# RWKV's triangular inverses from diagonal blocks of 16 rows, joined to 32 rows on TensorE

## The chip, the cores and the metric

The kernel runs on one core of one Trainium2 chip. The metric is device time in microseconds (us), the median of several runs. The engines are named as in the profile: PE is TensorE (PEld its weight loads), DVE is VectorE, ACT is ScalarE, POOL is GpSimd, and SP issues DMAs.

## The reference

One encoder layer is computed for 256 tokens of width 2048 in float32: a normalisation, one wide projection, three mixers (gated MLP, Hyena long convolutions, RWKV-7 in both directions), a gated merge, an output projection and a feed-forward network. The change lies in the RWKV mixer alone. It has 16 heads of 64 channels, and for each head and direction this recurrence over the tokens:

```python
def step(s, inp):
    r_t, w_t, k_t, v_t, a_t, b_t = inp
    sa = jnp.einsum('dbhij,dbhj->dbhi', s, a_t)
    s = s * w_t[..., None, :] + sa[..., :, None] * b_t[..., None, :] + v_t[..., :, None] * k_t[..., None, :]
    return s, jnp.einsum('dbhij,dbhj->dbhi', s, r_t)
```

The kernel takes it in four chunks of 64 tokens. Inside a chunk the term with `sa` makes a triangular system I - M of 64 x 64, whose inverse is needed; between chunks a state of 64 x 64 for each head and direction is carried.

## The kernel before

Products with the large weights are "dense" steps: a piece of weights, 128 x 512, is loaded by SP into `w`, split by ACT into a high part `wh` (L225) and by DVE or POOL into a low part `wl` (L229), and PE then makes three matmuls for each 128 rows (L242, L243, L244, into `ps_dn`).

The RWKV stage goes over eight pairs of heads, j = 0 to 7. For each j five generators write code, and `threads` takes turns between them:

- `wkv_prep`: decays and scaled keys (`bk`, `ar`, `E`), with the scans on DVE (L555, L557) and products of POOL (L590 to L594);
- `wkv_scores`: score products on PE (L635), masked by DVE into `sc` (L637). ACT copies the 32 x 32 blocks on the diagonals into `Md` (L647), DVE transposes those of the second direction into `Mu` (L649), and SP writes both to a DRAM tile `d1`;
- `wkv_inverse`: it loads the 32 blocks of 32 x 32 back into `N` so that a block lies on one partition (four copies of the 32 blocks fill the 128 partitions), and inverts them by substitution. For each of 31 rows DVE makes one product into `Yt` (L688) and one sum into `Y` (L689), each quarter of the partitions for every fourth row of the result. `Y` goes to a DRAM tile `d2` and returns as `XX`, which DVE transposes (L702);
- `wkv_chain`: it joins the 32-row inverses to 64-row ones by two products (L731, an ACT copy L734, L742; DVE writes `xf`, L722 and L747), and then goes through the four chunks. Each has the products L770 (and L777 from the second chunk on) on PE, a copy `Pm` by DVE (L780), the product with the inverse L785, copies to `UV` (L791), state products L796, new state `sb` by DVE (L811, L813), and output products L816 and L819, summed in `y` (L826);
- `wkv_norm`: the group norm (L842, L843, ACT's L846, L848) and the gate.

After each turn in which a generator had something to do, `threads` puts dense steps into the code, about four for a round (12 matmuls): the projections of the j that come next (`front`), and, where the queue is short, the merge products of the Hyena branch. `need` puts in all that is left of a projection before the j that takes it. What is left when the generators are done is run behind them. `after` orders the generators among each other: the scores of j wait for the chain of j - 2, and a chain for its own inverse. The order of the instructions on each engine is then set by a scheduler, which takes the order of the code as priority and may move an instruction ahead of others that it holds to be late.

Of the kernel before, what the change touches and what calls it, by code (L numbers as in the profile page):

```python
# [9 lines left out]
F32 = mybir.dt.float32  # L10
# [6 lines left out]
P = 128  # L17
T = 256
D = 2048
KD = D // P  # L20
# [28 lines left out]
for _n, _w in VEC:  # L49
# [6 lines left out]
    ("smask", 256), ("dmask", 64), ("rowm", 2), ("scanm", 257),  # L56
# [11 lines left out]
def shape_constants():  # L68
    c = [np.zeros((P, NCST), np.float32), np.zeros((P, NCSW), np.float32)]

    def put(name, a):
        a = np.asarray(a, np.float32).reshape(P, -1)
        o, n, w = COFF[name]
        c[w][:, o:o + n] = a

    p = np.arange(P)
    put("ident", np.eye(P))
    put("bones", (p[:, None] // 64 == p[None, :] // 64) / 64.0)
    put("ones", np.full((P, P), 1.0 / D))
    put("unit", np.ones((P, P)))  # L80
    s = (p % 64)[:, None]
    t = np.arange(64)[None, :]
    put("smask", np.concatenate([s < t, s <= t, s > t, s >= t], 1))
    blk = (p // 32) % 2
    put("dmask", (np.arange(2)[None, :, None] == blk[:, None, None]) * np.ones((1, 1, 32)))
    put("rowm", np.stack([blk == 0, blk == 1], 1))
    put("scanm", np.broadcast_to((np.arange(T + 1) % CH != 0)[None], (P, T + 1)))
    lin = linspace01()
    put("negt", np.broadcast_to(-lin[None], (P, T)))
    return c  # L90
# [18 lines left out]
def dft_tables():  # L109
    """odd frequencies (2 k + 1) pi / (2 T), k < T / 2; even and odd samples apart"""  # L110
    n = np.arange(T).reshape(P, 2, 1, 1)
    k = np.arange(P)
    th = np.pi * (2 * k + 1) * n / (2 * T)
    fwd = np.concatenate([np.cos(th), -np.sin(th)], 2)
    inv = (fwd / T).transpose(3, 2, 1, 0)
    return tuple(np.ascontiguousarray(a.reshape(P, 512), dtype=np.float32) for a in (fwd, inv))
# [15 lines left out]
def layout(inp):  # L132
    g = {k: np.asarray(v) for k, v in inp.items()}
    o = {}
# [52 lines left out]
    o["rows"] = np.eye(32).reshape(8, 4, 32).transpose(1, 0, 2)[:, None] * np.ones((1, 32, 1, 1))  # L187
    o["rows"] = o["rows"].reshape(P, 8, 32)
# [5 lines left out]
class Build:  # L194
# [21 lines left out]
    # weights [P, nk, n] from DRAM -> (wh, wl)  # L216
# [16 lines left out]
    def dense(self, ap, xh, xl, ps):  # L233
        """ps[n, t] = sum_k w[k, n] x[k, t]; ap DRAM [P, nk, 128], xh/xl [P, nk, 256]; yields after each k"""
        mm = self.nc.tensor.matmul
        nk = ap.shape[1]
        for k0 in range(0, nk, KPIECE):
            k1 = min(nk, k0 + KPIECE)
            wh, wl = self.take(ap[:, k0:k1, :])
            for k in range(k0, k1):  # L240
                i = k - k0
                mm(ps, wh[:, i, :], xh[:, k, :], start=(k == 0), stop=False)  # L242
                mm(ps, wh[:, i, :], xl[:, k, :], start=False, stop=False)  # L243
                mm(ps, wl[:, i, :], xh[:, k, :], start=False, stop=(k == nk - 1))  # L244
                yield

    def dense_wide(self, ap, x, ps, whole=False):
        """as dense, in fewer passes: x(k) is [P, 2, 256], the two parts, and the sum of ps's halves the product;
        with whole it is in the first half"""
        mm = self.nc.tensor.matmul  # L250
        nk = ap.shape[1]
        for k0 in range(0, nk, KPIECE):
            k1 = min(nk, k0 + KPIECE)
            wh, wl = self.take(ap[:, k0:k1, :])
            for k in range(k0, k1):
                i = k - k0
# [12 lines left out]
    def take(self, ap):  # L269
        """the split weights; those that the plan has next are split ahead of their turn"""  # L270
# [6 lines left out]
    def feed(self, label, gen, aps):  # L277
        """gen takes the weights aps, [P, nk, 128] each, one after the other"""
# [4 lines left out]
    def fill(self, n):  # L283
        """emits n steps of the waiting dense products"""
# [26 lines left out]
    def rsqrt_steps(self, x, w, v):  # L311
        """w * -RS_B = x ** -0.5 (x > 0): bit estimate and two Newton steps"""
# [74 lines left out]
    def rwkv(self, rp, ych, ycl, y):  # L387
# [9 lines left out]
        # kd = k (1 + (a - 1) k_a) = k (ka1 (2 a - 1) + ka0)  # L397
# [19 lines left out]

        fronts = {}
# [15 lines left out]
        def more():  # L434
            """the next merge, the queue being short"""
# [45 lines left out]
    def threads(self, live, more):  # L481
        """takes turns between the generators, with dense steps between: more where fewer have something to do"""
# [19 lines left out]
    def weave(self, gens, steps, lead=0):  # L502
        """takes turns between the generators (a pair (n, gen) starts n turns late), with some of `steps` dense ones between"""
# [22 lines left out]
    def wkv_prep(self, R, j, front, res):  # L526
        """decay, a, normalised k; what scores and chain take; bonus and gate"""
# [11 lines left out]
        # cum = sum of sigmoid(w) from the chunk's edge, ta = 2 sigmoid(a) - 1  # L539
# [19 lines left out]
        # normalised kk, with its sign turned  # L559
# [39 lines left out]
        # bonus  # L599
# [18 lines left out]
    def wkv_scores(self, R, j, pre, sts):  # L618
        """scores of all chunks; transposed b, k; the blocks to invert"""
# [7 lines left out]
        # scores  # L627
# [11 lines left out]
        # the 32 x 32 blocks on the diagonals of M, upper (for d = 1 transposed)  # L639
# [10 lines left out]
        d1 = self.dp.tile([2, 4, P, 32], F32, tag="d1", name="d1", bufs=2)  # L650
        for d, z in enumerate((Md[:, 0, :], Mu)):
            nc.sync.dma_start(d1[d].rearrange("u p e -> p u e"), z.rearrange("p (u e) -> p u e", e=32))
        sts[j] = [sc, d1]
        self.passed.add(("blocks", j))
        yield 1
        # transposed b, k
# [10 lines left out]
    def wkv_inverse(self, R, j, st):  # L667
        """inverses of the diagonal 32 x 32 blocks of I - M, with a block on a partition: the partitions hold four times the
        32 blocks, each time with every fourth row of the inverses"""
        rp = R["rp"]  # L670
        V, D = self.nc.vector, self.nc.sync
        tl = lambda sh, name, bufs=1: rp.tile([P] + sh, F32, tag=name, name=name, bufs=bufs)
        mult, add = ALU.mult, ALU.add
        d1 = st[1]
        N = tl([32, 32], "N")
        yield 1
        src = d1.rearrange("d u (q s) e -> (d u q) (s e)", s=32)
        for i in range(4):
            D.dma_start(N[32 * i:32 * i + 32].rearrange("p s e -> p (s e)"), src)
        Y, Yt = tl([8, 32], "Y"), tl([80], "Yt")  # L680
# [3 lines left out]
        E = self.nc.vector  # L684
        for k in range(31):
            n, w = 31 - k, k // 4 + 1
            z = Yt[:, :w * n].rearrange("p (c t) -> p c t", t=n)
            E.tensor_tensor(z, N[:, k, k + 1:].unsqueeze(1).broadcast_to([P, w, n]), Y[:, :w, k:k + 1].broadcast_to([P, w, n]), mult)  # L688
            E.tensor_tensor(Y[:, :w, k + 1:], Y[:, :w, k + 1:], z, add)  # L689
            if k % 4 == 3:  # L690
                yield 1
        d2 = self.dp.tile([32, 8, 4, 32], F32, tag="d2", name="d2", bufs=2)
        for i in range(4):
            D.dma_start(d2[:, :, i, :], Y[32 * i:32 * i + 32])
        yield 1
        yield from self.after("whole", j - 1)
        # [transposed d = 0, inverse d = 1, inverse d = 0, transposed d = 1]
        XX = tl([4, P], "XX")
        D.dma_start(XX[:, :2].rearrange("p d (u e) -> p (d u) e", e=32), d2.rearrange("(u q) c r e -> (q c r) u e", q=4))
        yield 1  # L700
        yield 1
        V.transpose(XX[:, 2:].rearrange("p a b -> p (a b)"), XX[:, :2].rearrange("p a b -> p (a b)"))  # L702
# [4 lines left out]
    def wkv_chain(self, R, j, pre, st):  # L707
        """the inverses of the 64 x 64 blocks, the chain over chunks"""
# [7 lines left out]
        sc, _, bkT, XX = st  # L716
# [33 lines left out]
        # v in [t, channel] layout, next to where u will stand  # L750
# [11 lines left out]
        # chain over chunks  # L762
# [70 lines left out]
    def wkv_norm(self, R, j, pre, ych, ycl):  # L833
        """group norm, bonus and gate"""
# [28 lines left out]
    def filter_mlp(self, p, zs):  # L863
        """z3[hidden, t] of the implicit filters' network: high parts, and low parts below them"""
# [37 lines left out]
    def filter_weights(self, p, o, g):  # L902
        """high parts twice, for both parts of z3, and low parts; after the load"""
# [14 lines left out]
    def filter_block(self, p, z3, edec, o, g, nxt, out):  # L918
        """spectra (E + O, E - O of even and odd taps) of 256 channels' filters, the skip as a part of tap 0"""
# [56 lines left out]
    def plus_minus(self, p, out, ps):  # L976
        """out[:, 0 / 1] = ps[0] +- ps[1], [re, im] each"""
# [13 lines left out]
    def tables(self, p):  # L991
        """the transforms' tables and the first filters' weights"""
# [138 lines left out]
    def gmlp(self, p, yah, yal):  # L1131
        """spatial gating; its products take x g, their results the token's 1 / rms; on the way h, for the others"""
# [28 lines left out]
        # the functions' table is there before the first data  # L1161
# [101 lines left out]
    def merge_part(self, p, n, b, y, out, first):  # L1263
        """out[:, n] (+)= (1 + tanh(gate / 2)) (y w_branch): twice the branch's term"""
# [54 lines left out]
    def sumsq(self, p, acc, x, n):  # L1319
        """acc += x ** 2 (and the mean's epsilon), but for the last of the KD tiles, which is returned"""  # L1320
# [10 lines left out]
    def token_rstd(self, p, acc, nm, last):  # L1331
        """r * -RS_B is the tokens' 1 / rms"""
# [66 lines left out]
```

## Time and profile before

| what | value |
|---|---|
| median of 3 runs | 2072.45 us (2071.43 to 2075.77) |
| span of the profiled execution | 2081.1 us |
| PE, PEld busy | 95%, 85% |
| DVE, ACT, POOL busy | 71%, 49%, 27% |

The profile is one execution, whose span is 8.7 us above the median of the runs. A busy PE is not a PE at its peak: a matmul of 256 columns is shown with some 0.28 us though the next one starts 0.12 us after it. The RWKV stage, from the first matmul of its preparation to the last norm and the dense steps behind it, lies between 509 and 1110 us; before it come the gated MLP and Hyena, after it the merge, the output projection and the feed-forward network.

### The profile page before, as it was taken

The numbers are of one execution on the slowest core, as the hardware profiler recorded it, in microseconds if no ns is written. First come the engines' busy times: TensorE is split into PE (matmuls) and PEld (weight loads), VectorE is DVE, ScalarE is ACT, GpSimd is POOL, SyncE is SP. The second block draws the span as 40 slices with busy tenths as digits, with TensorE's granted clock in tenths as the row PEclk, the third lists the DMA queues.
The fourth block names the chain that finished last, engine by engine and source line by source line (L and its number), as shares of the span: only waits on it lengthen the run. The fifth ranks groups of instructions, "written<-read, shape, count | busy, mean of one in ns | idle before, by whom it ended". The sixth has DMA issues, their size and how long they took to land. (4 is left out here: it accounts for less than half of the span.)

```text
span 2081.1 us, 37899 instructions
## 1 busy us (share of the span) xinstructions
PE 1985.2 (95%) x13636; PEld 1762.9 (85%) x13636; DVE 1468.4 (71%) x2852; ACT 1020.5 (49%) x1982; POOL 552.9 (27%) x557
## 2 busy tenths in 40 slices
PE   7999999999888888999999999999999999999997
PEld 5899999999777777877778888888888888888886
DVE  7968788765887786776766667766666666655555
ACT  5655555545333343333335555555555555544543
POOL 5322322325643443453441121111111111100001
PEclk9999999999888999898899999999999999999998
DMA  7454444345332233332324556555555555566664
GB/s 235 153 173 151 133 161 150 127 157 175 121 103 84 86 106 94 106 103 74 107 91 161 186 197 219 186 191 189 192 189 191 189 190 190 190 186 187 186 187 137
DMA packets 200325, 324.35 MB, mean 156 GB/s; under 512 B 45766, under 2 KB 49352, under 8 KB 200136
## 3 DMA queue, kind: packets, MB, share of 16 engines
q1 hardware_dynamic: 193904, 310.33, 45.9%
q0 software_dynamic: 1888, 5.93, 0.9%
q10 hardware_dynamic: 4344, 5.67, 0.8%
q8 instruction: 107, 1.75, 0.4%
q14 instruction: 82, 0.67, 0.1%
HBM read 317.65 MB, written 4.19 MB: 155 GB/s over the span
## 5 line engine op out<-in xcount | busy, mean ns | idle before, releaser
L225 ACT CAST wh<-w 128x512 fp32r<-128x512 f32 x1148 | 705.0, 619 | 693.8 <-PE ps_dn L262 259.6
L229 DVE TENSOR_TENSOR wl<-w,wh 128x512 fp32r<-128x512 f32 x945 | 709.0, 755 | 370.0 <-ACT wh L225 366.2
L242 PE MATMUL ps_dn<-hw,wh 128*128 128x256 f32 x1328 | 407.4, 307 | 2.3 <-ACT th L1269 1.2
L229 POOL TENSOR_TENSOR wl<-w,wh 128x512 fp32r<-128x512 f32 x203 | 273.2, 1349 | 454.7 <-ACT wh L225 432.2
L244 PE MATMUL ps_dn<-hw,wl 128*128 128x256 f32 x1328 | 388.8, 293 | 1.3 <-DVE wl L229 1.3
L243 PE MATMUL ps_dn<-hw,wh 128*128 128x256 f32 x1328 | 389.7, 293 | 0.0
L242 PEld LDWEIGHTS ps_dn<-hw,wh 128*128 128x128 f32 x1328 | 264.5, 199 | 18.6 <-issue 8.5
L243 PEld LDWEIGHTS ps_dn<-hw,wh 128*128 128x128 f32 x1328 | 265.1, 200 | 4.3 <-issue 1.7
L244 PEld LDWEIGHTS ps_dn<-hw,wl 128*128 128x128 f32 x1328 | 264.7, 199 | 3.7 <-DVE wl L229 1.5
L262 PE MATMUL ps_dn<-gw,wh 128*128 128x512 f32 x704 | 246.3, 391 | 0.0
L262 PE MATMUL ps_big<-gw,wh 128*128 128x512 f32 x704 | 246.0, 391 | 0.0
L262 PE MATMUL ps_dn<-hid,wh 128*128 128x512 f32 x660 | 233.2, 396 | 0.0
L263 PE MATMUL ps_dn<-hid,wl 128*128 128x256 f32 x704 | 198.4, 282 | 0.0
L263 PE MATMUL ps_dn<-gw,wl 128*128 128x256 f32 x704 | 197.3, 280 | 0.0
L263 PE MATMUL ps_big<-gw,wl 128*128 128x256 f32 x704 | 197.1, 280 | 0.0
L262 PEld LDWEIGHTS ps_dn<-gw,wh 128*128 128x128 f32 x704 | 131.7, 187 | 28.9
L262 PEld LDWEIGHTS ps_big<-gw,wh 128*128 128x128 f32 x704 | 131.6, 187 | 28.9
L262 PEld LDWEIGHTS ps_dn<-hid,wh 128*128 128x128 f32 x660 | 124.0, 188 | 30.2
L263 PEld LDWEIGHTS ps_dn<-gw,wl 128*128 128x128 f32 x704 | 133.1, 189 | 0.1
L263 PEld LDWEIGHTS ps_big<-gw,wl 128*128 128x128 f32 x704 | 133.1, 189 | 0.0
L263 PEld LDWEIGHTS ps_dn<-hid,wl 128*128 128x128 f32 x704 | 132.2, 188 | 0.0
L1328 POOL TENSOR_TENSOR acc<-acc,sq 128x256 f32<-128x256 f32 x28 | 20.8, 744 | 291.3 <-ACT sq L1326 283.3
(383 smaller groups left out, 3499.0 us busy)
## 6 DMA issues: line engine op xcount, KB each, us to landing
w<-in_wgu_dram SPq DMA_DIRECT2D x352, 256.0 KB, 3.0
w<-in_wgt_dram SPq DMA_DIRECT2D x192, 256.0 KB, 3.0
w<-in_wdn_dram SPq DMA_DIRECT2D x176, 256.0 KB, 2.9
w<-in_wc_dram SPq DMA_DIRECT2D x108, 256.0 KB, 3.0
w<-in_wb_dram SPq DMA_DIRECT2D x96, 256.0 KB, 3.0
w<-in_wbr_dram SPq DMA_DIRECT2D x96, 256.0 KB, 2.7
w<-in_wo_dram SPq DMA_DIRECT2D x64, 256.0 KB, 3.1
w<-in_wav_dram SPq DMA_DIRECT2D x32, 256.0 KB, 3.9
```

Source lines behind the costliest of these rows:

```text
L225: nc.scalar.copy(wh[:, :m], w[:, :m])
L229: e.tensor_tensor(wl[:, :m], w[:, :m], wh[:, :m].bitcast(F32), ALU.subtract)
L242: mm(ps, wh[:, i, :], xh[:, k, :], start=(k == 0), stop=False)
L243: mm(ps, wh[:, i, :], xl[:, k, :], start=False, stop=False)
L244: mm(ps, wl[:, i, :], xh[:, k, :], start=False, stop=(k == nk - 1))
L262: mm(ps, wh[:, i, :], xk.rearrange("p a t -> p (a t)"), start=(k == 0), stop=False)
L263: mm(ps[:, :T], wl[:, i, :], xk[:, 0, :], start=False, stop=(k == nk - 1))
L1328: self.nc.gpsimd.tensor_tensor(acc, acc, s, ALU.add)
```

## The change

Blocks of 16 rows are inverted by substitution instead of blocks of 32. There are twice as many (64), and with each block on two partitions, one for the even and one for the odd rows of the result, they fill the 128 partitions again. The substitution has 15 steps of two DVE instructions instead of 31, on rows up to 15 elements long instead of 31.

With the two 16-row inverses on the diagonal of a 32 x 32 block in `Z`, its off-diagonal part is Z Mo Z, where `Mo` holds the 16 x 16 part of M above the diagonal. `Mo` is made by POOL in `wkv_scores`, two products with a mask. `Z` is transposed by DVE; 32 matmuls of 32 x 32 make the first product, ACT copies it into `T0`, 32 more make the second, and DVE adds it to `Z` into `XX`. This code has one more turn than before, and the substitution has three turns instead of seven.

The DRAM tile `d2` is now two tiles that live through the stage and are set to zero once, by two DMAs of POOL, since the parts off the diagonal are not written. `N` is loaded in rows of 16 elements (64 bytes) instead of whole blocks (4 KB a partition), and `Y` is stored in rows of 16 instead of 32 elements. The table `rows` is half as large.

```diff
 CSW = [
-    ("smask", 256), ("dmask", 64), ("rowm", 2), ("scanm", 257),
+    ("smask", 256), ("dmask", 64), ("rowm", 2), ("scanm", 257), ("omask", 32),
 ]
...
+        R["d2"] = [self.dp.tile([32, 2, 8, 2, 32], F32, name=f"d2{i}") for i in range(2)]
+        none = rp.tile([P, 256], F32, name="none", tag="kd")
+        nc.gpsimd.memset(none, 0.0)
+        for x in R["d2"]:
+            nc.gpsimd.dma_start(x.rearrange("a b c r e -> (a b c r e)").rearrange("(p f) -> p f", p=P), none)
...
         d1 = self.dp.tile([2, 4, P, 32], F32, tag="d1", name="d1", bufs=2)
+        Mo = tl([2, P], "Mo", 2)
         for d, z in enumerate((Md[:, 0, :], Mu)):
-            nc.sync.dma_start(d1[d].rearrange("u p e -> p u e"), z.rearrange("p (u e) -> p u e", e=32))
-        sts[j] = [sc, d1]
+            z = z.rearrange("p (u e) -> p u e", e=32)
+            nc.sync.dma_start(d1[d].rearrange("u p e -> p u e"), z)
+            G.tensor_tensor(Mo[:, d, :].rearrange("p (u e) -> p u e", e=32), z,
+                            self.cst("omask").unsqueeze(1).broadcast_to([P, 4, 32]), mult)
+        sts[j] = [sc, d1, Mo]
...
-        N = tl([32, 32], "N")
+        d1, Mo = st[1:3]
+        N = tl([16, 16], "N")
         yield 1
-        src = d1.rearrange("d u (q s) e -> (d u q) (s e)", s=32)
+        src = d1.rearrange("d u (q s) e -> (d u q) s e", s=32)
         for i in range(4):
-            D.dma_start(N[32 * i:32 * i + 32].rearrange("p s e -> p (s e)"), src)
-        Y, Yt = tl([8, 32], "Y"), tl([80], "Yt")
+            b = 16 * (i % 2)
+            D.dma_start(N[32 * i:32 * i + 32], src[:, b:b + 16, b:b + 16])
+        Y, Yt = tl([8, 16], "Y"), tl([40], "Yt")
...
-        for k in range(31):
-            n, w = 31 - k, k // 4 + 1
+        for k in range(15):
+            n, w = 15 - k, k // 2 + 1
...
-        d2 = self.dp.tile([32, 8, 4, 32], F32, tag="d2", name="d2", bufs=2)
+        d2 = R["d2"][j % 2]
         for i in range(4):
-            D.dma_start(d2[:, :, i, :], Y[32 * i:32 * i + 32])
+            r, b = i // 2, i % 2
+            D.dma_start(d2[:, b, :, r, 16 * b:16 * b + 16], Y[32 * i:32 * i + 32])
...
         XX = tl([4, P], "XX")
-        D.dma_start(XX[:, :2].rearrange("p d (u e) -> p (d u) e", e=32), d2.rearrange("(u q) c r e -> (q c r) u e", q=4))
+        Z = tl([2, 2, P], "Z")
+        D.dma_start(Z[:, 0].rearrange("p d (u e) -> p (d u) e", e=32), d2.rearrange("(u q) b c r e -> (q b c r) u e", q=4))
         yield 1
         yield 1
+        V.transpose(Z[:, 1].rearrange("p a b -> p (a b)"), Z[:, 0].rearrange("p a b -> p (a b)"))
+        blocks = [(d, u, q) for d in range(2) for u in range(4) for q in range(4)]
+        ps = self.pst("inv")
+        for d, u, q in blocks:
+            r, o = slice(32 * q, 32 * q + 32), slice(32 * u, 32 * u + 32)
+            nc.tensor.matmul(ps[r, P * d + 32 * u:P * d + 32 * u + 32], Mo[r, d, o], Z[r, 1, d, o], start=True, stop=True,
+                             tile_position=(32 * q, 32 * q))
+        T0 = tl([2, P], "T0")
+        S.copy(T0, ps[:, :2 * P].rearrange("p (d n) -> p d n", d=2))
+        yield 1
+        ps = self.pst("inv")
+        for d, u, q in blocks:
...
+        V.tensor_tensor(XX[:, :2], Z[:, 0], ps[:, :2 * P].rearrange("p (d n) -> p d n", d=2), add)
         V.transpose(XX[:, 2:].rearrange("p a b -> p (a b)"), XX[:, :2].rearrange("p a b -> p (a b)"))
```

The scheduler's order moves at three places. The lines of the changed kernel stand 1 to 30 further down (the dense matmuls L242 to L244 are its L243 to L245, L770 is L800, L785 is L815, L796 is L826).

PE, the inverses of j = 3 before the change: the 64-row products L731 and L742 stand behind the whole chain of j = 2, between the score products L635 of j = 4, and ahead of the first L785 of their own chain.

```order
L244 MATMUL ps_dn<-hw,wl 128x256
L635 MATMUL ps_big<-ar,bk 128x128 x4
L731 MATMUL ps_inv<-XX,sc 32x32 x16
L635 MATMUL ps_big<-ar,bk 128x128 x2
L742 MATMUL ps_inv<-XX,T_9710 32x32 x16
L635 MATMUL ps_big<-ar,bk 128x128 x2
L242 MATMUL ps_dn<-hw,wh 128x256
L243 MATMUL ps_dn<-hw,wh 128x256
L785 MATMUL ps_ch<-Pm,xf 64x64
```

PE now, the inverses of j = 3: the first new product, with `Z`, stands inside the last step of the chain of j = 2.

```order
L243 MATMUL ps_dn<-hw,wh 128x256
L721 MATMUL ps_inv<-Z,Mo 32x32 x32
L244 MATMUL ps_dn<-hw,wh 128x256
L245 MATMUL ps_dn<-hw,wl 128x256
L243 MATMUL ps_dn<-hw,wh 128x256
L244 MATMUL ps_dn<-hw,wh 128x256
L245 MATMUL ps_dn<-hw,wl 128x256
L815 MATMUL ps_ch<-Pm,xf 64x64 x4
```

What waits for the loaded inverse on PE now has a step of another chain (L815) and dense matmuls behind it; for j = 1, 5 and 7 it is the same, for even j the first product stands behind the chain that goes before.

PE, the second step of the chain of j = 6 before the change: the state products L796, and the next that takes the new state `sb`, L777.

```order
L796 MATMUL ps_ch<-UV,bkT 64x64 x4
L243 MATMUL ps_dn<-hw,wh 128x256
L244 MATMUL ps_dn<-hw,wl 128x256
L242 MATMUL ps_dn<-hw,wh 128x256
L243 MATMUL ps_dn<-hw,wh 128x256
L244 MATMUL ps_dn<-hw,wl 128x256
L242 MATMUL ps_dn<-hw,wh 128x256
L243 MATMUL ps_dn<-hw,wh 128x256
L244 MATMUL ps_dn<-hw,wl 128x256
L777 MATMUL ps_ch<-sb_6470,ar 64x128
```

PE now, the same step, from the state product L826 on: none of what is shown takes the new state.

```order
L826 MATMUL ps_ch<-UV,bkT 64x64 x4
L243 MATMUL ps_dn<-hw,wh 128x256
L244 MATMUL ps_dn<-hw,wh 128x256
L245 MATMUL ps_dn<-hw,wl 128x256
L243 MATMUL ps_dn<-hw,wh 128x256
L244 MATMUL ps_dn<-hw,wh 128x256
L245 MATMUL ps_dn<-hw,wl 128x256
L243 MATMUL ps_dn<-hw,wh 128x256
L244 MATMUL ps_dn<-hw,wh 128x256
L245 MATMUL ps_dn<-hw,wl 128x256
L243 MATMUL ps_dn<-hw,wh 128x256
L244 MATMUL ps_dn<-hw,wh 128x256
```

Eight dense matmuls stood between the state product and the one that takes the new state; now there are eleven, and what follows them are the outputs of the same step, which take the old state.

DVE, behind the last sum of the substitution of j = 2 before the change, up to the transpose of the loaded inverses (`UV` and `Pm` begin the chain of j = 2, `cum` is the preparation of j = 4).

```order
L689 TENSOR_TENSOR Y<-Y,Yt 128x8
L384 SCALAR_TENSOR_TENSOR v<-ps_dn,vecs,v 128x255
L229 TENSOR_TENSOR wl<-w,wh 128x512
L385 SCALAR_TENSOR_TENSOR v<-ps_dn,vecs,v 128x255
L758 COPY UV<-ps_big 64x4x128
L780 COPY Pm<-ps_ch 128x128
L384 SCALAR_TENSOR_TENSOR rk_8818<-ps_dn,vecs,rk_8818 128x255
L385 SCALAR_TENSOR_TENSOR rk_8818<-ps_dn,vecs,rk_8818 128x255
L553 TENSOR_SCALAR tw<-tw 128x256
L555 SCALAR_TENSOR_TENSOR cum<-wconsts,tw 128x256
L702 STREAM_TRANSPOSE XX<-XX 128x256
```

DVE now, at the same place (`bk`, `rk` and `ar` belong to the preparation of j = 3, `y` to the chain of j = 1):

```order
L701 TENSOR_TENSOR Y<-Y,Yt 128x8
L599 SCALAR_TENSOR_TENSOR bk<-ta,kk 128x2x128
L598 SCALAR_TENSOR_TENSOR ta<-ta,cum 128x256
L610 SCALAR_TENSOR_TENSOR rk<-rk_8229,vecs,rk 128x256
L599 SCALAR_TENSOR_TENSOR bk<-ta,kk 128x2x128
L856 TENSOR_TENSOR y_8350<-y_8350,ps_ch 128x64 x2
L1305 SCALAR_TENSOR_TENSOR th<-th,ps_dn 128x256
L602 TENSOR_TENSOR ar<-rk_8229,E 128x4x64 x2
L873 TENSOR_TENSOR y_8350<-y_8350,ps_big 128x256
L716 STREAM_TRANSPOSE Z<-Z 128x256
```

The way from `Y` over DRAM back to the first transpose has about as much other DVE work beside it as before, ten instructions instead of nine; but the work now belongs to the chain and the preparations that run on.

## Rows read from the trace of the kernel before

**Rows 1.** The page: busy time of each engine (share of the span, instructions).

```profile
PE 1985.2 (95%) x13636; PEld 1762.9 (85%) x13636; DVE 1468.4 (71%) x2852; ACT 1020.5 (49%) x1982; POOL 552.9 (27%) x557
```

**Rows 2.** Windows: RWKV stage, then the rest; busy us of each engine, granted clock.

```profile
core 0: us, PE busy (x) PEld busy (x) DVE busy (x) ACT busy (x) POOL busy (x), PEclk, DMA share, GB/s
509.00:1110.00 601.00, 540.20 (x4459) 461.92 (x4458) 449.57 (x1152) 218.70 (x479) 265.46 (x256) 0.90 0.32 99
1110.00:2070.00 960.00, 957.49 (x5518) 839.79 (x5516) 626.87 (x1032) 517.07 (x969) 108.26 (x140) 1.00 0.58 188
```

**Rows 3.** Windows: the eight stretches of the stage with a substitution on DVE; one, sum.

```profile
690.00:736.00 46.00, 38.36 (x297) 34.09 (x292) 41.36 (x113) 14.65 (x32) 21.72 (x24) 0.93 0.22 71
...
sum 335.00, PE 291.50 PEld 250.47 DVE 283.10 ACT 108.36 POOL 156.86; mean PE 36.44 PEld 31.31 DVE 35.39 ACT 13.55 POOL 19.61
```

**Rows 4.** Windows: the nine stretches of the stage between them; the last, and the sum.

```profile
1061.00:1110.00 49.00, 47.28 (x435) 39.85 (x436) 26.11 (x63) 18.58 (x41) 16.10 (x15) 0.97 0.36 109
sum 266.00, PE 248.70 PEld 211.45 DVE 166.48 ACT 110.33 POOL 108.60; mean PE 27.63 PEld 23.49 DVE 18.50 ACT 12.26 POOL 12.07
```

**Rows 5.** Waits of PE in the stage, longest in total first: us, times, longest us.

```profile
PE ps_big L848 <- ACT sq L846: 9.4, 5, 3.4
PE ps_ch L770 <- DVE UV L758: 9.3, 5, 3.8
PE ps_ch L777 <- DVE sb L811: 7.4, 6, 2.3
PE ps_big L635 <- DVE sc L637: 7.0, 3, 3.1
PE ps_ch L816 <- DVE sb L811: 6.1, 6, 1.9
PE ps_big L605 <- DVE rk L603: 5.7, 2, 3.3
PE ps_inv L731 <- DVE XX L702: 2.3, 4, 1.0
```

**Rows 6.** Groups by line: the substitution. Busy us, mean ns, then idle before it.

```profile
L689 DVE TENSOR_TENSOR Y<-Y,Yt 128x60 f32<-128x60 f32 (+24 forms) x248 | 95.1, 383 | 4.0
L688 DVE TENSOR_TENSOR Yt<-N,Y 128x60 f32<-128x60 f32 (+24 forms) x248 | 92.7, 374 | 3.7
```

**Rows 7.** Timelines of DVE and of POOL, 565 to 571 us: start, us, instruction.

```profile
565.39 4.89 DVE L688 TENSOR_TENSOR Yt<-N,Y 128x30 f32<-128x30 f32 x1
570.32 0.19 DVE L689 TENSOR_TENSOR Y<-Y,Yt 128x30 f32<-128x30 f32 x1
...
567.73 2.49 POOL L229 TENSOR_TENSOR wl<-w,wh 128x512 fp32r<-128x512 f32 x2
```

**Rows 8.** Timeline of PE at a 64-row join (each matmul has two records).

```profile
610.60 0.45 PE L731 MATMUL ps_inv<-XX,sc 32*32 32x32 f32 x32 [0.53 <-DVE XX L702]
610.98 0.39 PE L243 MATMUL ps_dn<-hw,wh 128*128 128x256 f32 x1
611.21 0.28 PE L244 MATMUL ps_dn<-hw,wl 128*128 128x256 f32 x1
```

**Rows 9.** Groups by line: the nearest to the new instructions of DVE, ACT and POOL.

```profile
L594 POOL TENSOR_TENSOR ar<-kk,E 128x256 f32<-128x256 f32 x16 | 11.3, 728 | 10.7 <-PE ps_ch L819 10.7
L702 DVE STREAM_TRANSPOSE XX<-XX 128x256 f32<-128x256 f32 x8 | 3.5, 437 | 2.8 <-DMA XX<-d 2.8
L610 ACT COPY gg<-ps_big 128x256 f32<-128x256 f32 x8 | 3.0, 370 | 9.4 <-DVE bon L608 9.4
```

**Rows 10.** DMA issues: count, KB of each, median us from issue to landing.

```profile
N<-d SPq DMA_DIRECT2D x32, 128.0 KB, 3.4
...
d<-Y SPq DMA_DIRECT2D x32, 32.0 KB, 2.0
XX<-d SPq DMA_DIRECT2D x8, 128.0 KB, 3.3
...
d<-Md SPq DMA_DIRECT2D x8, 64.0 KB, 1.8
```

More of the change, by code (lines that the diff above doesn't have):

```diff
@@ L86, in shape_constants @@
     put("rowm", np.stack([blk == 0, blk == 1], 1))
+    put("omask", (p[:, None] % 32 < 16) & (np.arange(32)[None] >= 16))
     put("scanm", np.broadcast_to((np.arange(T + 1) % CH != 0)[None], (P, T + 1)))
@@ L186, in layout @@
     o["cst"], o["csw"] = shape_constants()
-    o["rows"] = np.eye(32).reshape(8, 4, 32).transpose(1, 0, 2)[:, None] * np.ones((1, 32, 1, 1))
-    o["rows"] = o["rows"].reshape(P, 8, 32)
+    o["rows"] = np.eye(16).reshape(8, 2, 16).transpose(1, 0, 2)[:, None] * np.ones((1, 64, 1, 1))
+    o["rows"] = o["rows"].reshape(P, 8, 16)
     o["feat"] = filter_features()
@@ L667, in wkv_inverse @@
     def wkv_inverse(self, R, j, st):
+        nc = self.nc
         rp = R["rp"]
-        V, D = self.nc.vector, self.nc.sync
+        V, S, D = nc.vector, nc.scalar, nc.sync
         tl = lambda sh, name, bufs=1: rp.tile([P] + sh, F32, tag=name, name=name, bufs=bufs)
         mult, add = ALU.mult, ALU.add
-        d1 = st[1]
-        N = tl([32, 32], "N")
+        d1, Mo = st[1:3]
+        N = tl([16, 16], "N")
         yield 1
-        src = d1.rearrange("d u (q s) e -> (d u q) (s e)", s=32)
+        src = d1.rearrange("d u (q s) e -> (d u q) s e", s=32)
         for i in range(4):
-            D.dma_start(N[32 * i:32 * i + 32].rearrange("p s e -> p (s e)"), src)
-        Y, Yt = tl([8, 32], "Y"), tl([80], "Yt")
+            b = 16 * (i % 2)
+            D.dma_start(N[32 * i:32 * i + 32], src[:, b:b + 16, b:b + 16])
+        Y, Yt = tl([8, 16], "Y"), tl([40], "Yt")
         D.dma_start(Y, self.t["rows"])
@@ L683, in wkv_inverse @@
         yield 1
-        E = self.nc.vector
-        for k in range(31):
-            n, w = 31 - k, k // 4 + 1
+        for k in range(15):
+            n, w = 15 - k, k // 2 + 1
             z = Yt[:, :w * n].rearrange("p (c t) -> p c t", t=n)
-            E.tensor_tensor(z, N[:, k, k + 1:].unsqueeze(1).broadcast_to([P, w, n]), Y[:, :w, k:k + 1].broadcast_to([P, w, n]), mult)
-            E.tensor_tensor(Y[:, :w, k + 1:], Y[:, :w, k + 1:], z, add)
+            V.tensor_tensor(z, N[:, k, k + 1:].unsqueeze(1).broadcast_to([P, w, n]), Y[:, :w, k:k + 1].broadcast_to([P, w, n]), mult)
+            V.tensor_tensor(Y[:, :w, k + 1:], Y[:, :w, k + 1:], z, add)
             if k % 4 == 3:
                 yield 1
-        d2 = self.dp.tile([32, 8, 4, 32], F32, tag="d2", name="d2", bufs=2)
+        d2 = R["d2"][j % 2]
         for i in range(4):
-            D.dma_start(d2[:, :, i, :], Y[32 * i:32 * i + 32])
+            r, b = i // 2, i % 2
+            D.dma_start(d2[:, b, :, r, 16 * b:16 * b + 16], Y[32 * i:32 * i + 32])
         yield 1
@@ L698, in wkv_inverse @@
         XX = tl([4, P], "XX")
-        D.dma_start(XX[:, :2].rearrange("p d (u e) -> p (d u) e", e=32), d2.rearrange("(u q) c r e -> (q c r) u e", q=4))
+        Z = tl([2, 2, P], "Z")
+        D.dma_start(Z[:, 0].rearrange("p d (u e) -> p (d u) e", e=32), d2.rearrange("(u q) b c r e -> (q b c r) u e", q=4))
         yield 1
         yield 1
+        V.transpose(Z[:, 1].rearrange("p a b -> p (a b)"), Z[:, 0].rearrange("p a b -> p (a b)"))
[10 more added lines that the diff above has]
+        for d, u, q in blocks:
+            r, o = slice(32 * q, 32 * q + 32), slice(32 * u, 32 * u + 32)
+            nc.tensor.matmul(ps[r, P * d + 32 * u:P * d + 32 * u + 32], T0[r, d, o], Z[r, 0, d, o], start=True, stop=True,
+                             tile_position=(32 * q, 32 * q))
+        V.tensor_tensor(XX[:, :2], Z[:, 0], ps[:, :2 * P].rearrange("p (d n) -> p d n", d=2), add)
         V.transpose(XX[:, 2:].rearrange("p a b -> p (a b)"), XX[:, :2].rearrange("p a b -> p (a b)"))
@@ L715, in wkv_chain @@
         v, E, bk, ar = pre[:4]
-        sc, _, bkT, XX = st
+        sc, _, _, bkT, XX = st
         units = [(d, c, h) for h in range(2) for cp in range(2) for d in range(2) for c in (2 * cp, 2 * cp + 1)]
```

## The prediction

> **What bounds the kernel now.** I read the page's busy times first: PE 95%, DVE 71% of the span [rows 1]. That is a mean over stages, so the second view is the table by windows. Behind 1110 us PE is busy 957.5 of 960 us at the full clock of 2.4 GHz, and nothing of the change is there [rows 2]. The RWKV stage is different: 601 us with PE busy 540.2, so 60.8 us idle, at a granted clock of 0.90, which means that a fifth of the stage ran at the lower level of 1.2 GHz and 601 x 0.10 = 60 us of matmul time were lost by it. What the change can give is in these two sums; PE's own work stays.
>
> The third view cuts the stage. From the first to the last DVE instruction of each j's substitution (L688, L689) eight stretches make up 335 us. In them PE idles 335 - 291.5 = 43.5 us, or 13.0%, and DVE is busy 283.1 us, or 85% [rows 3]. Between them lie 266 us, where PE idles 17.3 us, 6.5%, and DVE is busy 63% [rows 4]. PE's waits say the same: what ends most of them is DVE, late with a state (L811), a mask (L637), a copy (L758) or what ACT makes of its result (L846) [rows 5]. None of these is the substitution itself; it is what stands in DVE's queue before them. So the stage ends by PE's work, plus waits on a crowded DVE, plus the clock.
>
> **The change part by part.**
>
> *DVE, removed.* The substitution costs 95.1 + 92.7 = 187.8 us in 496 instructions, 379 ns each [rows 6]. An undisturbed one of 30 elements takes 0.19 us, while the one before it took 4.89 us: it ended as POOL ended the instructions it was in the midst of [rows 7]. At 0.2 us each 496 would take 99 us, so 89 us of the group are such delays, 0.18 us for each instruction. Now there are 8 x 30 = 240, of about the size of the short ones: 240 x 0.19 = 46 us, and with the same delay each 43 us more. Freed: 187.8 - 89 = 99 us. Added: a transpose of 437 ns [rows 9] and a sum from PSUM for each j, which I take at the same: 8 x 0.87 = 7 us. Net 92 us of DVE's 450 in the stage. None of this is on PE's path by itself; what counts is what PE waits less.
>
> *PE's waits, the gain.* The low bound is by rates: the stretches shrink with the instructions, 335 x 240 / 496 = 162 us, and 173 us get the idle rate of the others: 173 x 0.065 = 11 us. The high bound is that all 43.5 us of the stretches go. The order speaks for more than the low bound: a chain's step that had eight dense matmuls to cover the new state now has eleven and the outputs. Over the stage, of the 24 places where PE goes from the state product to the next that takes the state, 12 had less than 1.2 us of own work between, and one has it now; for L785 to L796 it was 8 of 24, and is 3. These are the places of the 7.4 and 6.1 us [rows 5]. The other four large rows, 31.4 us, keep their cover and only gain by the shorter queue. I take the middle, -27 us.
>
> *The clock.* It falls behind stretches in which PE idles or runs small matmuls, so it follows the idle time, but not surely: small matmuls stay. Bounds 0 and 27 us (60 us lost for 60.8 idle); the middle, -14.
>
> *PE, added.* 512 matmuls of 32 x 32, in 16 blocks of 32. A block of 16 holds PE from 610.60 to 610.98, 0.38 us, and the dense one behind it takes 0.39 instead of 0.28 [rows 8]. So 16 x (0.76 + 0.11) = 13.9 us, and at the stage's clock 13.9 / 0.90 = 15. All of it counts, since PE is the engine that the stage ends by. Bounds 12 to 20.
>
> *New waits.* For each j PE now meets four waits instead of two: L721 for `Z`, L729 for ACT's copy, then the old two behind the sum and the transpose. The old one cost 2.3 us for all j [rows 5]. ACT's copy takes 0.37 us [rows 9], and the order puts 4 to 15 dense matmuls (0.5 to 1.8 us) beside it, so four of the eight places are short by some tenths of a us. Bounds 0 and 10 us, taken +4, near the old row. What waits behind L721 on PE is the rest of the chain of j - 1 where j is odd; that is the slower rival below.
>
> *Queues.* POOL gets two products of 128 x 128 for each j, half of a row of 728 ns [rows 9]: 16 x 0.4 = 6 us on an engine busy 265 of 601 us [rows 2]. They wait for ACT's `Md` and DVE's `Mu`, and splits of weights stand behind them, at most a few tenths of a us each, since POOL waits mostly for ACT itself. On SP the count of DMAs is the same. Their landing: 64 KB in rows of 128 bytes lands in 1.8 us, 128 KB of such rows in 3.3, and the present load of `N`, in whole blocks, in 3.4 [rows 10]. The new load has 2,048 rows of 64 bytes for each j, so I bound it by the 1.8 us of 512 rows for each of its four DMAs and twice the 3.3 us of 1,024 rows: -1.6 to +3.2 us, with the generator two turns ahead of its use. Taken as nothing. The two DMAs that clear `d2` run once, ahead of the stage's first use; nothing, or one landing of 3 us.
>
> The Trainium skill (DMA: Bandwidth & Descriptors, Specifications) says that a transfer below 512 B is written by read and modify, which speaks against the 64-byte rows. By the rows of 128 bytes, which land no later than whole blocks, the trace does not show it as a delay; rows of 64 bytes it has none of that size to show, so it is a rival below.
>
> *Moved behind.* By the order, PE has 2,130 dense matmuls between the stage's first product and its last norm, now 2,076; 54 go behind it. That is PE's work at either place: nothing.
>
> **Sum.** -27 - 14 + 15 + 4 = -22 us. The profiled execution would go from 2081.1 to 2059; its span is 8.7 us above the median of the runs, and I carry the difference over: 2072.45 - 22 = **2050 us**.
>
> **The rivals.**
>
> *The stage was held by the two-j loop of chain and inverse, and all its idle time goes.* Scores wait for the chain of j - 2, the inverse for the scores, the chain for the inverse; the substitution is some 42 us of each turn of that loop, and halves. For it: 13% against 6.5% idle. Against it: PE idles between the stretches too, and is busy 97% in the last one, in which no substitution runs [rows 4]. Then up to 43.5 + 8 us of idle and 40 of the clock go: -92 + 19 = -73, 2000 us; the case covers 1995 to 2036.
>
> *The DVE time was not DVE's.* If POOL's instructions hold back whatever two-input instruction DVE has next, the delays do not fall with the count; they move to masks, sums and splits that stand next. Then only 240 of 496 undisturbed times go, PE gains the low bound, 11 us of idle and 5 of the clock, against 19 added: +3, about 2075, within 2070 to 2078. For it speaks the 4.89 us row; against it, that with 256 fewer instructions DVE meets POOL less often.
>
> The Trainium skill (Advanced Engine Details and Errata, VectorE Performance Modes) has DVE's second port shared with GpSimd, so that the two block each other. It names DVE's two-port modes; the row here is a float32 product of two operands. By that rule the time would be this rival's if POOL's work sets the delay.
>
> *PE waits inside a chain (slower).* L721 stands in the last step or middle of the chain of j - 1 for j = 1, 3, 5 and 7. Before it come the stores of `Y` (2.0 us) and the load of `Z` (3.3 us) [rows 10], so at least 5.3 us after the last sum, with some ten DVE instructions beside. If PE has to wait it out, 4 x 5.3, and half of it for even j, 4 x 2.6, make 32 us, and the clock gains nothing: -27 + 15 + 32 = +20, 2092 us; the case covers 2077 to 2095. It decides where PE waits more than (27 + 14 - 15) / 8 = 3.3 us for each j. Against it: before, PE waited 2.3 us in all for the same way over DRAM.
>
> *Small rows land late.* If `N` landed the full 3.2 us later and each j's inverse with it, at most 8 x 3.2 = 26 us would come back: 2076.
>
> That the change doesn't do what it says is not open: the counts by the order are 240 and 512.
>
> **How the numbers follow.** Forecast 0.46 (2036 to 2062); all idle time goes 0.20; delays not DVE's 0.14; PE waits in the chain 0.16; late rows 0.04. Within 0.2%, 4.1 us, is about what a measurement of this kernel can tell from no change, the runs lying 4.3 us apart. Of the delays' case 0.09 falls within it and 0.05 above, of the late rows' 0.02 and 0.02. So faster 0.46 + 0.20 = 0.66, same 0.09 + 0.02 = 0.11, slower 0.16 + 0.05 + 0.02 = 0.23. From 2005 to 2080 about 0.06 is left out below and 0.13 above.
>
> **What would show it.** PE busy in the stage should rise by some 10 us or less while its idle time falls from 60.8 to 30 to 40 and the clock rises to 0.92 or more; the two groups of the substitution together should be near 90 us in 240 instructions; the stretches some 20 us each. PE's waits for L811 should shrink most; waits at L721 and L729 should stay below 6 us together. I would be wrong by the first step if the stretches shrink and PE's idle time does not; by the price of the products if a block of 32 holds PE for more than 1 us; and by the clock if idle time falls and the granted clock does not rise.

## The result and the profile after

The changed kernel takes 2048.05 us, median of 4 runs (2046.48 to 2053.64), against 2073.57 us (2071.43 to 2075.77): a ratio of 0.9882, with a 95% interval of 0.9853 to 0.9911. The forecast was 2050. The profiled execution has a span of 2044.6 us. That is 3.4 us below the median of its runs, while the profile of the kernel before lies 8.7 us above its own; so differences between the two traces are too large for the change: 36.5 us between the spans, 25.5 between the medians.

The page, against [rows 1]:

```profile
PE 1964.6 (96%) x14660; PEld 1751.7 (86%) x14660; DVE 1398.1 (68%) x2612; ACT 1022.1 (50%) x1990; POOL 567.5 (28%) x576
```

PE has 1,024 records more (512 matmuls, two records each) and is busy 20.6 us less. This is the first thing to read: a busy time grows and shrinks with the clock. The windows, the RWKV stage first, against [rows 2]:

```profile
core 0: us, PE busy (x) PEld busy (x) DVE busy (x) ACT busy (x) POOL busy (x), PEclk, DMA share, GB/s
503.00:1074.00 571.00, 523.77 (x5478) 452.60 (x5477) 379.89 (x912) 220.60 (x487) 275.18 (x273) 0.93 0.34 96
1074.00:2035.00 961.00, 956.57 (x5526) 840.18 (x5524) 627.77 (x1035) 517.32 (x969) 109.51 (x141) 1.00 0.59 188
```

The stage is 571 us instead of 601, the rest is the same. PE's idle time in the stage fell from 60.8 to 571 - 523.8 = 47.2 us. The granted clock rose from 0.90 to 0.93, so what the lower level of 1.2 GHz takes fell from 60 to 571 x 0.07 = 40 us. The remaining 6 us between the two spans lie ahead of the stage, which begins at 509 us in the one and at 503 in the other; in the kernels below it begins at 505 to 509, with the change or without it.

The stretches with a substitution on DVE, and those between them, as sums, against [rows 3] and [rows 4]:

```profile
sum 161.00, PE 136.48 PEld 113.39 DVE 137.91 ACT 49.30 POOL 75.99; mean PE 17.06 PEld 14.17 DVE 17.24 ACT 6.16 POOL 9.50
sum 410.00, PE 387.29 PEld 339.21 DVE 241.98 ACT 171.30 POOL 199.20; mean PE 43.03 PEld 37.69 DVE 26.89 ACT 19.03 POOL 22.13
```

The stretches halve, 335 to 161 us, but inside them PE idles 24.5 us, 15.2%, where it was 13.0%. Between them it idles 22.7 us, 5.5% instead of 6.5%. PE's waits in the stage, against [rows 5]:

```profile
PE ps_ch L846 <- DVE sb L841: 7.4, 6, 2.0
PE ps_big L612 <- DVE rk L610: 6.1, 2, 3.3
PE ps_ch L846 <- DVE sb L843: 5.6, 4, 2.4
PE ps_big L642 <- ACT gg L617: 5.0, 1, 5.0
PE ps_ch L800 <- DVE UV L788: 4.6, 2, 3.8
PE ps_big L878 <- ACT sq L876: 3.3, 2, 2.2
PE ps_inv L721 <- DVE Z L716: 2.5, 2, 1.6
PE ps_inv L729 <- ACT T L724: 1.6, 2, 1.3
```

The waits of L777 (now L807) for the state are gone, but the outputs L816 (now L846) wait 13.0 us for the instructions that write it. Before, they waited 8.1 us: 6.1 [rows 5] and this row.

```profile
PE ps_ch L816 <- DVE sb L813: 2.0, 1, 2.0
```

Those of the norm (L848, now L878) and of the first products of a chain (L770, now L800) shrank from 9.4 and 9.3 to 3.3 and 4.6. The new products wait 4.1 us in all. The groups of the substitution and of the new products, against [rows 6]:

```profile
L700 DVE TENSOR_TENSOR Yt<-N,Y 128x30 f32<-128x30 f32 (+10 forms) x120 | 45.4, 378 | 11.9 <-DMA N<-d 9.5
L701 DVE TENSOR_TENSOR Y<-Y,Yt 128x30 f32<-128x30 f32 (+10 forms) x120 | 37.1, 309 | 2.6
...
L729 PE MATMUL ps_inv<-Z,T 32*32 32x32 f32 x512 | 6.3, 199 | 1.6 <-ACT T L724 1.6
L721 PE MATMUL ps_inv<-Z,Mo 32*32 32x32 f32 x512 | 6.0, 194 | 2.5 <-DVE Z L716 2.5
```

### The profile page after: what moved, and what is told of

Same layout as the page of the kernel before. It is cut to its first block, busy times and chain, and to the rows that moved or that the text cites. A ratio compares the mean times of both kernels' runs of the same rounds, so it can differ in the third digit from the quotient of the medians.

```text
span 2044.6 us, 39736 instructions
## 1 busy us (share of the span) xinstructions
PE 1964.6 (96%) x14660; PEld 1751.7 (86%) x14660; DVE 1398.1 (68%) x2612; ACT 1022.1 (50%) x1990; POOL 567.5 (28%) x576
## 5 line engine op out<-in xcount | busy, mean ns | idle before, releaser
L243 PE MATMUL ps_dn<-hw,wh 128*128 128x256 f32 x1328 | 405.8, 306 | 2.1 <-ACT th L1299 1.2
L245 PE MATMUL ps_dn<-hw,wl 128*128 128x256 f32 x1328 | 382.8, 288 | 1.3 <-DVE wl L230 1.3
L244 PE MATMUL ps_dn<-hw,wh 128*128 128x256 f32 x1328 | 382.7, 288 | 0.0
L243 PEld LDWEIGHTS ps_dn<-hw,wh 128*128 128x128 f32 x1328 | 259.6, 195 | 20.8 <-issue 10.0
L244 PEld LDWEIGHTS ps_dn<-hw,wh 128*128 128x128 f32 x1328 | 260.4, 196 | 2.1 <-issue 0.5
L245 PEld LDWEIGHTS ps_dn<-hw,wl 128*128 128x128 f32 x1328 | 260.0, 196 | 2.5 <-DVE wl L230 1.5
```

## The experiments

My theory: DVE's time, freed by half the steps, brings less idle time of PE and, behind it, more clock; the products take some of it back. The rivals: the order of the turns brings it; POOL's delays stay and move to other instructions. Each ratio below is to the kernel before, on the same chip.

**Half the steps, nothing else.**

```diff
-        for k in range(31):
-            n, w = 31 - k, k // 4 + 1
+        for k in range(15):
+            n, w = 15 - k, k // 2 + 1
...
-            if k % 4 == 3:
+            if k % 2 == 1:
                 yield 1
```

> The kernel before, its substitution cut to 15 steps on rows of up to 15 elements (240 instead of 496 DVE instructions), with a turn behind every second step so that the seven turns stay. It leaves out half of each inverse, and has none of the new products, waits or the other tables. If the gain is DVE's freed time and the clock behind it (my theory: -27 and -14), it is 41 us faster than before, 2032. If POOL's delays only move to DVE's other instructions, 16 us faster, 2057. If the gain is the changed order of turns, within 4 us of before.

Measured: 2025.66 us, ratio 0.9748 (0.9713 to 0.9783), so 52 us faster (45 to 59), 11 more than my theory had it. The stage by windows:

```profile
506.00:1051.00 545.00, 504.23 (x4452) 437.59 (x4452) 369.33 (x895) 218.76 (x479) 263.62 (x256) 0.94 0.37 109
```

DVE is busy 80 us less. PE idles 40.8 us, 20 less; the clock takes 545 x 0.06 = 33 us, 27 less. The two make 47 of the 56 us by which the stage is shorter in these traces; where the other 9 went is not shown.

**The same with three turns.** Here `k % 4 == 3` stays as it was.

> As the kernel with half the steps, but with a turn behind every fourth step, three instead of seven, as in the changed kernel. It leaves out half of each inverse. If DVE's time alone counts, the same as with seven turns within 4 us; if the fewer turns (the cover that they put behind the chain's state products) bring the gain, 15 to 25 us faster than with seven turns.

Measured: 2035.47 us, ratio 0.9795 (0.9757 to 0.9832), 42 us faster.

```profile
505.00:1056.00 551.00, 503.22 (x4444) 436.56 (x4444) 371.30 (x895) 218.41 (x478) 262.94 (x256) 0.94 0.36 107
```

The fewer turns bring no gain; they may cost some (the intervals overlap).

**The changed kernel with seven turns**, `k % 2 == 1` instead of `k % 4 == 3`.

> The changed kernel with a turn behind every second step of the substitution, seven instead of three, as before the change; nothing else. If the gain is DVE's time, the same as the changed kernel within 4 us. If it is the order, 10 to 25 us of the gain are gone, 2058 to 2073.

Measured: 2045.16 us, ratio 0.9842 (0.9805 to 0.9878); the changed kernel's is 0.9882 (0.9853 to 0.9911). No difference that the runs can tell. By both runs the gain does not come from the order of the turns.

**DVE filled up again.**

```diff
             V.tensor_tensor(Y[:, :w, k + 1:], Y[:, :w, k + 1:], z, add)
+            V.tensor_tensor(Yt[:, :w * n], Yt[:, :w * n], Yt[:, :w * n], ALU.max)
+            V.tensor_tensor(Yt[:, :w * n], Yt[:, :w * n], Yt[:, :w * n], ALU.max)
```

> The changed kernel with two more DVE instructions behind each of the 15 steps of the substitution (a maximum of Yt with itself, of the same size, in place; nothing takes it): 480 instead of 240 for the whole stage, near the 496 of before, the turns unchanged. If the gain comes from DVE's time, this gives back what the halved substitution brought, 40 to 50 us: about 2092, slower than before by 15 to 20. If it comes from the order of the instructions on PE, it stays within 5 us of the changed kernel.

Measured: 2075.43 us, ratio 0.9987 (0.9966 to 1.0009): the whole gain is gone.

```profile
506.00:1097.00 591.00, 531.89 (x5476) 457.90 (x5476) 435.22 (x1152) 222.63 (x487) 273.98 (x273) 0.92 0.34 93
```

DVE's 55 us more in the stage cost about 22 us by the ratios. That is about half of what I expected, and less for each us than in the two runs above: 0.4 here, 42 / 78 = 0.54 and 52 / 80 = 0.65 there. Instructions of DVE alone, with the turns unchanged, are thus shown to move the kernel's time.

**The products taken out.** The two blocks of matmuls and the copy `T0` are left out, and the last sum takes `Z[:, 1]` instead of `ps`.

> The changed kernel without the two product blocks and ACT's copy; the loaded Z is summed with its transpose in the place of the last sum. It leaves out the part of each inverse off the diagonal. By my sum the products are 15 us and their two waits some of the 4: 16 us faster than the changed kernel, 2032. By the difference between the changed kernel and the half-step kernel with as few turns (20 us in the stage), 2028, if nothing but the products and their waits lies between the two; if the way over DRAM in small rows or POOL's new products count too, less than 10 us.

Measured: 2026.79 us, ratio 0.977 (0.9739 to 0.9801), 1.1% or 23 us below the changed kernel.

```profile
509.00:1061.00 552.00, 507.68 (x4481) 439.56 (x4480) 387.15 (x918) 220.91 (x485) 274.64 (x273) 0.94 0.36 101
```

The stage is 19 us shorter than the changed kernel's and as long as with half the steps and three turns (551): the small rows, the longer-lived `d2` and POOL's new products cost nothing that shows. Of the 19, PE's busy time gives 16 (at a clock of 0.94 instead of 0.93) and its idle time 3.

**The products twice**, `for d, u, q in 2 * blocks` at both places.

> The changed kernel with each of its 16 blocks of 32 new matmuls issued twice, into the same tile. My price is 0.87 us for a block, 13.9 us at full clock, 15 at the stage's: 2063, 0.7% slower than the changed kernel. If the blocks lie beside waits, less than 5 us; if they cost more than they show (the clock falls behind small matmuls), over 20.

Measured: 2074.43 us, ratio 0.9993 (0.9965 to 1.0022), 23 us above the changed kernel. That is the same price once more, but not for the same reason. The timeline of PE, changed kernel first, then the products twice:

```profile
703.87 0.75 PE L721 MATMUL ps_inv<-Z,Mo 32*32 32x32 f32 x64 [0.86 <-DVE Z L716]
704.55 0.39 PE L243 MATMUL ps_dn<-hw,wh 128*128 128x256 f32 x1
```

```profile
582.22 1.29 PE L721 MATMUL ps_inv<-Z,Mo 32*32 32x32 f32 x128 [0.94 <-DVE Z L716]
583.44 0.39 PE L244 MATMUL ps_dn<-hw,wh 128*128 128x256 f32 x1
...
584.11 0.79 PE L729 MATMUL ps_inv<-Z,T 32*32 32x32 f32 x69
587.50 1.06 PE L729 MATMUL ps_inv<-Z,T 32*32 32x32 f32 x59 [2.61 <-issue]
588.49 0.58 PE L245 MATMUL ps_dn<-hw,wl 128*128 128x256 f32 x1
588.87 0.41 PE L243 MATMUL ps_dn<-hw,wh 128*128 128x256 f32 x1
589.09 0.41 PE L244 MATMUL ps_dn<-hw,wh 128*128 128x256 f32 x1
```

A block holds PE for 0.75 us, doubled 1.29. But the second block of a doubled pair stops in its midst, for nothing that the profile shows, and behind it the dense matmuls follow one another at 0.2 instead of 0.12 us, the lower clock. PE's waits give the sum:

```profile
PE ps_inv L729 <- issue: 11.4, 7, 2.6
```

So 11.4 of the 23 us are stops that the single blocks don't have. This run bounds the price from above; the run without the products gives it.

**No splits on POOL**, in the RWKV stage of the kernel before, and of the changed kernel.

```diff
-        self.pool_share = 0.6
+        self.pool_share = 0
         self.threads([norms(), chains(), inverses(), scores(), preps()], more)
+        self.pool_share = 0.6
```

> The kernel before with all splits of weights in the RWKV stage on DVE: POOL's 142 go there, 0.78 us each, +111 us. If POOL's work sets the delays of the substitution, its mean falls from 379 ns towards 250, -64 us for its 496 instructions, and the masks and sums lose some 20 more: DVE gets 25 us busier, and the time rises by 3 to 15 us. If the delays are not POOL's, the mean stays and the time rises by over 40.

> The changed kernel with all splits of weights in the RWKV stage on DVE. If POOL's work sets the delays, the substitution's mean falls from 344 to 250 ns, -23 us for 240 instructions, other lines lose up to 40, and DVE gets 50 us busier: 10 to 30 us slower than the changed kernel. If the delays are not POOL's, over 40.

Measured: the kernel before 2019.93 us, ratio 0.9738 (0.9706 to 0.9771), 54 us faster; the changed one 1996.84 us, ratio 0.9621 (0.9587 to 0.9656). I had expected both to be slower. The stage and DVE's costliest groups, the kernel before (the edit moves each line one further down, so the substitution is L689 and L690 here, L701 and L702 below):

```profile
508.00:1049.00 541.00, 505.09 (x4466) 427.39 (x4465) 418.76 (x1297) 218.78 (x480) 85.66 (x114) 0.96 0.38 111
```

```profile
L229 DVE TENSOR_TENSOR wl<-w,wh 128x512 fp32r<-128x512 f32 x188 | 131.7, 702 | 15.7 <-ACT wh L225 12.2 <-PE ps_dn L263 2.7 <-PE ps_dn L244 0.2
L689 DVE TENSOR_TENSOR Yt<-N,Y 128x60 f32<-128x60 f32 (+24 forms) x248 | 54.9, 222 | 1.6
L690 DVE TENSOR_TENSOR Y<-Y,Yt 128x60 f32<-128x60 f32 (+24 forms) x248 | 54.4, 220 | 1.8
```

And the changed kernel:

```profile
506.00:1016.00 510.00, 496.67 (x5470) 429.76 (x5469) 392.13 (x1053) 221.67 (x486) 95.18 (x130) 0.99 0.39 107
```

```profile
L701 DVE TENSOR_TENSOR Yt<-N,Y 128x30 f32<-128x30 f32 (+10 forms) x120 | 25.4, 211 | 3.2 <-DMA Y<-in_rows_dram 0.9 <-DMA N<-d 0.7 <-DVE y L857 0.2
L702 DVE TENSOR_TENSOR Y<-Y,Yt 128x30 f32<-128x30 f32 (+10 forms) x120 | 24.9, 208 | 1.6
```

The same instructions of the substitution take 0.22 instead of 0.38 us. DVE has 144 instructions of splits more, and is yet busy 31 us less than in [rows 2]. So the delays come with POOL's splits, and on the substitution they were 187.8 - 109.3 = 78.5 us before and 82.5 - 50.3 = 32.2 us after the change. Most instructions have none: in the changed kernel L700 takes 0.19 us on the median and 2.50 at most, without POOL's splits 0.18 and 0.75. PE's idle time in the changed kernel falls to 13.3 us and the clock rises to 0.99. DVE is busy 12 us more there than with POOL's splits, 392.1 against 379.9, and the kernel is still 2.6% faster. So DVE's busy time alone is not what PE waits for. That it is the few long instructions, which hold up what stands behind them, fits these numbers; no run shows it by itself. The change itself gives the same ratio here, 0.9621 / 0.9738 = 0.988.

**Between, and with seven turns.** The changed kernel with `pool_share` 0.25 in the stage, and with 0 and `k % 2 == 1`.

> The changed kernel with a quarter of the splits of the RWKV stage on POOL instead of 0.6. If POOL holds DVE back in proportion to its own work, the time lies on the line between 1997 (none) and 2049 (0.6): 2019. If a part of POOL's work lies beside DVE's for nothing and the best share is between, below 1997.

> The changed kernel with all splits of weights in the RWKV stage on DVE and with seven turns in the substitution instead of three. PE idled only 13 us in the stage without POOL's splits and lost 7 us of clock, so the order has little left to give: within 5 us of the kernel with three turns, 1997. If the turns set how much cover stands behind a state product also here, 5 to 10 us lie between the two.

Measured: 2011.88 us, ratio 0.9692 (0.9665 to 0.9719), between none and 0.6 and a little below the line of 2019, so a quarter is no better than none; and 2001.63 us, ratio 0.965 (0.9622 to 0.9677), the same as with three turns.

**The outputs in a tile of their own.** The wait at L846 was still to be explained: the outputs take the old state, so they need not wait for the new one. But they write the PSUM tile `ct` that the state products stand in, and DVE reads these from there (L841, L843).

```diff
+            po = self.pst("inv")
             for d, c, h in us:
-                o = ct[64 * h:64 * h + 64, 64 * d:64 * d + 64]
+                o = po[64 * h:64 * h + 64, 64 * d:64 * d + 64]
```

> The changed kernel with the output products of the chain (L846, L849) written to a PSUM tile of their own, taken from the two of ps_inv, instead of to the ps_ch tile that the state products stand in. If the outputs wait for DVE's new state only because they write the tile that DVE still reads, the 13.0 us of PE's waits there go; with some clock behind them (0 to 13 us) and other waits that come late next, the kernel gets 5 to 20 us faster, 2028 to 2043. If the sharing of ps_inv with the joins makes new waits as long, no change within 4 us.

> The same with all splits of weights in the RWKV stage on DVE. PE idles 13 us in that stage without the edit, and waits below 1 us for the state, so the edit can give nearly nothing here: 1993 to 2000, within 4 us of 1997.

Measured: 2033.91 us, ratio 0.9792 (0.9764 to 0.9821), 0.9% or 19 us below the changed kernel; without POOL's splits 1994.25 us, ratio 0.9605 (0.9567 to 0.9642), the same as without the edit. The stage of the first, and its longest waits:

```profile
507.00:1063.00 556.00, 512.99 (x5477) 447.64 (x5476) 383.23 (x912) 221.09 (x488) 274.34 (x272) 0.94 0.35 99
```

```profile
PE ps_inv L721 <- DVE Z L716: 7.5, 5, 4.2
PE ps_ch L826 <- ACT UV L821: 6.4, 7, 1.3
PE ps_big L612 <- DVE rk L610: 6.1, 2, 3.3
PE ps_big L642 <- ACT gg L617: 5.0, 1, 5.0
PE ps_ch L800 <- DVE UV L788: 3.7, 2, 2.9
PE ps_inv L847 <- DVE UV L821: 3.1, 3, 1.4
```

Of PE's waits for the state 0.2 us are left; the outputs (L847) now wait 3.1 us for a copy. So the 13 us were the shared tile's. PE's idle time fell by 4.2 us only, 47.2 to 43.0, because the waits at L721, L826 and L847 grew; its busy time fell by 10.8, 523.8 to 513.0, with the clock at 0.94 instead of 0.93. The 19 us are what the edit gives in all, and most of them do not show as idle time. Without POOL's splits such waits were 0.8 us, and the edit gives nothing. The fastest versions are these two without POOL's splits, 1994 and 1997 us, which the runs can't tell apart.

## Why the prediction was right, and where its steps were off

The sum held, -22 against -25 us, and both its sides held: half the steps with as few turns brought 42 us, where idle time and clock together were put at 41; products and their waits cost 23 us (19 in the stage), where they were put at 15 + 4. Inside the first side the shares were wrong, so that the sum came out within 4 us is in part luck: the waits gave less than I had put, and in the traces the clock gave more.

- *PE's waits, -27.* Measured -13.6 net. The new products' waits, a term of their own, are 4.1 us of the 47.2 that are left, so 17.7 us of the old ones went; the idle time did not reach the 30 to 40 us that I had named as a sign. The step that failed is the one by which the order "speaks for more" than the low bound of 11. Behind the longer cover L777 waits no more, but the outputs L846 wait 4.9 us longer. I had counted those as cover because they take the old state, and had not looked at where they write: into the tile that DVE reads the state product from, as the run with a tile of their own shows. The runs on the turns show no gain from their order.
- *The clock, -14.* Measured -20 in the two traces, and -27 with half the steps alone, more than the idle time gave. The clocks of all runs on record give less: span times (1 - clock) is 64 us on the mean of 54 runs of the kernel before and 52 of the four of the changed one, so about 12, near the term. Idle time and clock moved together over the profiles, 60.8 us idle at 0.90, 47.2 at 0.93, 40.8 at 0.94, 35.9 at 0.96, 13.3 at 0.99, but not strictly: 59.1 us (DVE filled up) and 54.0 (products twice) went with 0.92, and 50.0 (seven turns) with 0.95. Small matmuls stand ahead of a fall too: in the kernel before PE ran scores, joins and chain products from 933 to 937 us, busy 3.90 of 4 us at a clock of 1.00, and the next 12 us, 11.69 of them busy, had 0.51.
- *DVE.* The substitution was put at 89 us and is 82.5. Its delay for each instruction fell a little, 78.5 / 496 = 0.16 to 32.2 / 240 = 0.13 us. Of the net 92 us, 89 went by the sum of DVE's groups, 498.6 to 409.5; by the windows, where overlapping records count once, it is 70.
- *The rival "the DVE time was not DVE's"* had its mechanism right: POOL's work sets the delay, as the runs without POOL's splits show. Its conclusion was wrong, because the delays fell with the count. Few moved: DVE's other groups, without the new L716 and L731 (6.8 us), rose by 9 us in all. The product L595 went from 684 ns, 10.9 us in all, to the first of these rows in the changed kernel; the second is that kernel without POOL's splits. The Trainium skill (GPSIMD Engine Reference, Key points) has DVE contend with GpSimd also in instructions "with two SBUF inputs"; these rows agree, for float32 operands.

```profile
L602 DVE TENSOR_TENSOR ar<-rk,E 128x256 f32<-128x256 f32 x16 | 13.7, 869 | 0.5 <-ACT E L582 0.5
```

```profile
L603 DVE TENSOR_TENSOR ar<-rk,E 128x256 f32<-128x256 f32 x16 | 7.7, 483 | 0.0
```

- *Products.* 0.75 us for a block, put at 0.76. PE's busy time did not rise, as I had asked of it, because the clock rose with it; the runs with and without the products, 523.8 and 507.7 us, show the 16, the clock's part in it included.
- *New waits.* L721 and L729 wait 4.1 us and L761 1.8, put at +4; the slower rival, PE held inside a chain, needed 3.3 us for each j and got 0.7.
- *Small rows.* The new load of `N`, a quarter of the bytes, lands in 3.1 us, the old one in 3.4 [rows 10]:

```profile
N<-d SPq DMA_DIRECT2D x32, 32.0 KB, 3.1
```

DVE waits 9.5 us for it in all, where the half-step kernel with three turns, which loads whole blocks, waits 0.3. The landing is no later, and why the wait is there is not shown; on PE's path nothing of it shows.

What stays open: why the doubled second block stops, whether the fewer turns cost the half-step kernel the 10 us between the two medians, and what of DVE's work PE waits for, if not its busy time.

## What to carry to other kernels

Instructions taken off a crowded engine beside the bound one, or added to it, moved the kernel by 0.4 to 0.65 of their time here, partly as waits and partly through the clock; the work that replaced them on the bound engine cost at least its full time (16 blocks of 0.75 us, 23 us in the kernel). But busy time is no measure across kernels: without POOL's splits the changed kernel had more of it on DVE and was faster. Before an engine's instructions are made fewer, look at why each takes as long as it does: where short ones take twice their undisturbed time on the mean, moving the neighbour that holds them can be worth more; here it was 54 us against 25. Where an order is to cover a wait, look at the tiles that an instruction writes as well as at what it reads.

## What the runs showed of the hardware that I had not expected

Work handed to POOL to relieve DVE made the kernel slower, and in the kernel before even DVE busier. The splits on either engine in the stage, the kernel before:

```profile
L229 POOL TENSOR_TENSOR wl<-w,wh 128x512 fp32r<-128x512 f32 x142 | 188.2, 1330 | 210.3 <-ACT wh L225 202.6 <-PE ps_dn L244 6.6
```

```profile
L229 DVE TENSOR_TENSOR wl<-w,wh 128x512 fp32r<-128x512 f32 x44 | 34.4, 781 | 7.7 <-ACT wh L225 7.5
```

One takes POOL 1.33 us and DVE 0.78, or 0.70 where POOL has none. With all on DVE its busy time fell from 449.6 to 418.8 us and the kernel got 54 us faster; in the changed kernel DVE's busy time rose by 12 us, and the kernel got faster by as much. The Trainium skill (Perfetto Trace Analysis, Optimizing Scalar/DVE Operations) warns that moving work between those two "might not help"; here it cost 2.6%.

Two blocks of 64 matmuls of 32 x 32, close behind one another, brought PE to stops of up to 2.6 us within the second, with nothing awaited that the profile shows. Among the changed kernel's waits, with 32 in each, there is no such row.
